# Router products turned round onto 32-column tiles, an older price table for the build-time scheduler, and an earlier start on the first tile's last affine step

## The chip, the cores and the metric

One core of one Trainium2 chip runs the whole network in a single launch. The metric is the device time of that core in microseconds (us), as the median of several runs; the profile is of one execution more. A core has the engines TensorE (PE in the profile, its weight loads PEld), VectorE (DVE), ScalarE (ACT), GpSimd (POOL) and SyncE (SP), which issues most of the DMAs.

## What is computed

The input is `x`, 256 tokens by 1024 numbers. Four layers follow: softmax attention with a dense feed-forward part, a short convolution with a dense feed-forward part, a gated linear recurrence with a mixture of experts, and a stick-breaking attention with a mixture of experts. The two mixtures matter here. For each token the reference computes 20 router logits, picks one of four expert groups and the best two experts in it, and sums these experts' outputs:

```
def post_norm(x, y, g, b):
    return layer_norm(DEEPNORM_ALPHA * x + y.astype(x.dtype), g, b)
...
    probs_g = jax.nn.softmax((xf @ w_group + b_group).astype(jnp.float32), axis=-1)
    p_top, g_idx = lax.top_k(probs_g, 1)
    logits_e = (xf @ w_router + b_router).astype(jnp.float32).reshape(T, N_GROUPS, EXPERTS_PER_GROUP)
...
    h = silu(x @ w_gate) * (x @ w_up);  y = (h * gates) @ w_down
```

After the second mixture comes the last `post_norm`, whose result is the output.

## The kernel before, in words

The 256 tokens are two tiles, T = 0 and T = 1, of 128 each. All weights stream from memory as units of 128 x 1024 numbers (512 KB) into a ring of 34 slots; `pump` (L537) issues their DMAs on SP as slots come free. Weights of dense stages are split by ACT and DVE into a rounded part `hi` and a rest `lo` (`prep_task`), and each product is three matmuls: activations' high part with both, low part with `hi`. The expert weights are used as they come ("raw").

**The order of the work** is made when the program is built. Every stage of each tile is a generator that emits instructions and yields its conditions; `Sched.run` (L269) always resumes the ready generator of lowest priority number, at a time that it keeps itself. That time comes from a table: `mm` (L451) adds a price for a matmul, `tr` (L463) one for a transpose, `onA` and `onD` those of ACT and DVE work, and `pump` says when a unit will have landed, with a fixed distance between units. On the chip nothing of this table is left but the order in which each engine and each DMA queue gets its instructions; an engine runs them in that order and waits on semaphores. So a changed price can move instructions anywhere in the program.

**Router.** `router` (L1370) folds the norm's gain into the router weights, `self.wr` (128 x 8 x 20), and its shift into `self.cr`. When a tile's output projection has made half b of its 1024 columns (`residual_half`, L1274, with a DVE statistics step), `front_half` (L1856) transposes these four blocks of 128, copies them to SBUF on ACT, and multiplies: for each of four blocks the transposed 128 x 128 block is the stationary operand and the 128 x 20 weights move, all eight blocks adding up in one PSUM bank. `moe_front` (L1875) then normalises `x` on DVE, forms the logits from the bank with two DVE steps, chooses the experts, ranks the tokens and builds the selection matrix; then `gather` and the experts' `gate_up` and `down` follow (`moe_task`). Tile 1 goes through its front last, while PE has tile 0's gather and first expert products.

**The end.** `down_last(1, 1)` (L2064) makes the last expert output of tile 1: matmuls, then an ACT copy and a DVE step for its two parts; `combined_last` (L2086) adds them into tile 1's bank. In `moe` (L2135) a tile's final norm begins with DVE statistics of its two banks and a power on POOL (`rstd`). Tile 0 then waits for the event `fin`, which tile 1 sets after its own statistics, and goes through `affine_pool` (L1304): a DVE step for -mean/deviation, two ACT passes of 128 x 512, gain and shift of its first half on POOL (two steps) with a DMA from ACT's queue, and after the event `sent` the same of its second half on DVE with a DMA from SP. Tile 1 uses `affine_rows` (L1289): four DVE steps of 128 x 512, and two DMAs from SP.

Of the kernel before, what the change touches and what calls it, by code (L numbers as in the profile page):

```python
# [8 lines left out]
F32 = mybir.dt.float32  # L9
# [3 lines left out]
ALU = mybir.AluOpType  # L13
# [288 lines left out]
class Body:  # L302
# [148 lines left out]
    def mm(self, out, lhsT, rhs, start, stop, shared=False):  # L451
        self.nc.tensor.matmul(out, lhsT, rhs, start=start, stop=stop, skip_group_check=shared)  # L452
        n = 1
        for d in rhs.shape[1:]:
            n *= d
        m = out.shape[0]
        if lhsT.dtype == F32R:
            c = max(0.227 * n / 512, 0.108)
        else:
            c = max(0.86 * n / 512, 0.224 if m > 64 else 0.112) * (0.26 if m <= 32 and n == 512 else 0.52 if m <= 64 and n == 512 else 1.0)  # L460
        self.sch.now += c

    def tr(self, out, in_):  # L463
        self.nc.tensor.transpose(out, in_, self.ident)  # L464
        self.sch.now += 0.109

    def act(self, out, in_, func, bias=0.0, scale=1.0, accum_out=None):
        want = {AF.Exp: "natural_log_exp_and_others", AF.Ln: "natural_log_exp_and_others", AF.Silu: "silu_and_others"}.get(func)
# [68 lines left out]
    def pump(self):  # L537
        while self.can_dma():
            i = self.nextdma
            if i == 4 and not self.again:  # L540
                self.nc.sync.dma_start(self.x[0], self.x_d[0])
                self.dma_t += 1.46
                self.x0_t = self.dma_t + 2.0
            if i == 18 and not self.again:
                self.nc.sync.dma_start(self.x[1], self.x_d[1])
                self.nc.sync.dma_start(self.cst, self.consts_d[:, 128:])
                self.dma_t += 2.3
                self.x1_t = self.dma_t + 2.0
            if self.plan.kind[i] == "row":
                t = self.ring.tile([128, 1024], F32, tag="u", name="row")  # L550
                r = self.rows_d[self.where[self.plan.src[i]]]
                self.nc.sync.dma_start(t, bass.AP(tensor=r.tensor, offset=r.offset, ap=[[0, 128], [1, 1024]]))
            else:
                t = self.ring.tile([128, 1024], F32, tag="u", name="raw")
                self.nc.sync.dma_start(t, self.units_d[self.where[self.plan.src[i]]])
            self.tiles[i] = t
            self.dma_t = max(self.dma_t, self.sch.now) + 1.3
            self.arr[i] = self.dma_t + 2.0
            if self.plan.kind[i] != "dense":
                self.ready[i] = self.arr[i]  # L560
            self.raw_used += 1
            if self.plan.kind[i] == "dense":
                self.rawdense += 1
            self.nextdma += 1
# [65 lines left out]
    def setup(self):  # L630
        nc = self.nc
        c = self.const
# [13 lines left out]
        self.stat = [c.tile([128, 4], F32, name=f"stat{t}") for t in range(2)]  # L646
        self.gtr = [c.tile([128, 32], F32R, name=f"gtr{t}") for t in range(2)]
        self.bns = [c.tile([128, 12], F32, name=f"bns{t}") for t in range(2)]
        self.wr = c.tile([128, 8, 20], F32, name="wr")
        self.cr = c.tile([128, 40], F32, name="cr")  # L650
        self.sel4 = c.tile([128, 1], F32, name="sel4")
        nc.gpsimd.memset(self.sel4, 0.0)
# [651 lines left out]
    def affine_pool(self, T, nm, src):  # L1304

        x, sv = self.x[T], self.stat[T]
        rows = self.rows(nm)
        yield [self.unit(r) for r in rows]
        nb = self.tm(1)
        self.ts(nb, sv[:, 0:1], sv[:, 2:3], -1.0, ALU.mult, ALU.mult)  # L1310
        for b in range(2):
            c = slice(b * 512, (b + 1) * 512)
            self.act(x[:, c], src[b], AF.Identity, bias=nb, scale=sv[:, 2:3])
        ops = list(zip((ALU.mult, ALU.add), [self.tiles[r] for r in rows]))
        for op, r in ops:
            self.nc.gpsimd.tensor_tensor(x[:, :512], x[:, :512], r[:, :512], op)
        self.nc.scalar.dma_start(self.out_d[T][:, :512], x[:, :512])
        yield f"sent{nm}"
        for op, r in ops:
            self.tt(x[:, 512:], x[:, 512:], r[:, 512:], op)  # L1320
        self.send(T, slice(512, 1024))
        for r in rows:
            self.done(r)
# [46 lines left out]
    def router(self, layer):  # L1370

        g, b_ = self.lncols(f"m{layer}")
        yield [self.bk(1), self.rH(1)]
        h = self.tH()
        t = h[:, :160].rearrange("p (k n) -> p k n", k=8)
        W = h[:, 160:320].rearrange("p (k n) -> p k n", k=8)
        self.nc.gpsimd.dma_start(h[:, 160:320], self.vecs_d[:, V_R + 160 * layer:V_R + 160 * layer + 160])
        yield 5.0
        self.tt(self.wr, W, g.unsqueeze(2).to_broadcast([128, 8, 20]), ALU.mult)
        self.tt(t, W, b_.unsqueeze(2).to_broadcast([128, 8, 20]), ALU.mult)  # L1380
        q = h[:, 320:360]
        self.red(q[:, :20], self.wr.rearrange("p k n -> p n k"), ALU.add)
        self.red(q[:, 20:], t.rearrange("p k n -> p n k"), ALU.add)
        yield self.w()
        bank = self.bank()
        self.mm(bank[:, :20], self.cst[:, C_NONE:C_NONE + 128], q[:, :20], True, True)
        self.mm(bank[:, 20:40], self.ones.bitcast(F32), q[:, 20:], True, True)
        self.vcopy(self.cr[:, :20], bank[:, :20])
        self.tt(self.cr[:, 20:], bank[:, 20:40], self.vecs[:, V_RB + 20 * layer:V_RB + 20 * layer + 20], ALU.add)
        self.free()  # L1390
        self.fH()
# [464 lines left out]
    def front_half(self, T, b, layer):  # L1856

        if b == 0:
            yield [self.bk(2), self.rS(1), ("t", self.ut[T][b])]
            self.xT[T] = self.tS().rearrange("p (k t) -> p k t", k=8)  # L1860
            self.lgb[T] = self.bank()
        else:
            yield [f"fh{layer}_{T}_0", self.bk(1), ("t", self.ut[T][b])]
        xT, lgb = self.xT[T], self.lgb[T]
        bank = self.bank()
        for j in range(4):
            self.tr(bank[:, j * 128:(j + 1) * 128], self.x[T][:, (4 * b + j) * 128:(4 * b + j + 1) * 128])
        self.scopy(xT[:, 4 * b:4 * b + 4].rearrange("p a b -> p (a b)"), bank)
        self.free()
        yield self.w()  # L1870
        for k in range(4 * b, 4 * b + 4):
            self.mm(lgb[:, :20], xT[:, k], self.wr[:, k], k == 0, k == 7)
        self.sch.set(f"fh{layer}_{T}_{b}")

    def moe_front(self, T, layer):  # L1875
# [15 lines left out]
            self.pump()  # L1891
        yield ("t", tl)
        lg = self.tm(20)
        self.stt(lg, self.cr[:, :20], sv[:, 0:1], bank[:, :20], ALU.mult, ALU.add)
        self.stt(lg, lg, sv[:, 2:3], self.cr[:, 20:], ALU.mult, ALU.add)
        self.free()
        gts, mk = self.gts[:, T], self.mks[:, T]
# [237 lines left out]
    def moe(self, T, layer):  # L2135
# [12 lines left out]
            self.onD(512)  # L2148
        self.stats(T, st)
        if T == 0 and self.last[T]:  # L2150
            yield f"fin{layer}"
            yield from self.affine_pool(T, f"f{layer}", acc)
        else:
            self.sch.set(f"fin{layer}")
            yield from self.affine_rows(T, f"f{layer}", acc)
            self.sch.set(f"sentf{layer}")
        self.free(2)
# [125 lines left out]
```

## Time and profile before

| | |
|---|---|
| median of 3 runs | 1204.48 us (1203.82 to 1207.32) |
| profiled execution, its own time | 1204.19 us |
| its span, first to last instruction | 1202.4 us |
| mean granted TensorE clock | 0.988 of full speed |
| busy: PE, DVE, ACT, POOL | 1144.9, 725.0, 549.1, 44.8 us |
| read and written | 298.83 and 2.10 MB |

Busy time of an engine is the union of its instructions; a matmul's record reaches from its start to the (modelled) end of its result, so neighbours overlap, and the pace of PE is read from the distance of two starts. "128*64" in a row is the part of the array that an instruction uses. What stands in brackets at the end of a row is the idle time just before it and what ended it.

### The profile page before, as it was taken

How to read it: one execution, taken by the hardware profiler on the slowest of the kernel's cores; microseconds unless marked ns; L12 is line 12 of the kernel's file. 1: busy time of each engine (PE TensorE's matmuls, PEld its weight loads, DVE VectorE, ACT ScalarE, POOL GpSimd, SP SyncE). 2: the span in 40 equal slices, each digit the busy share in tenths (PEclk: the TensorE clock that was granted, in tenths of full speed). 3: DMA queues.
4: the chain of work that ended last, by engine and by line, in shares of the span. 5: the costliest groups of instructions: out<-in, count | busy, mean ns of one | idle time of the engine just before them, and what ended most of it. 6: DMA issues, size and time to landing. Idle time of an engine off the chain costs nothing. (4 is left out here: it accounts for less than half of the span.)

```text
span 1202.4 us, 16685 instructions
## 1 busy us (share of the span) xinstructions
PE 1144.9 (95%) x6344; PEld 823.7 (69%) x6344; DVE 725.0 (60%) x1121; ACT 549.1 (46%) x913; POOL 44.8 (4%) x65
## 2 busy tenths in 40 slices
PE   7999989999998999999999999999999899999995
PEld 4777768888886787788887789886333577673331
DVE  4577667667577987665556567678221766564214
ACT  4655465434446455544434484553121456631211
POOL 0021000000000000000000000100000100000001
PEclk9999999999999999999999999999999899999998
DMA  9976768777664866466556233377999842587994
GB/s 375 409 306 228 256 222 302 262 268 269 244 239 155 340 247 215 158 211 217 205 194 209 86 125 105 123 277 266 378 409 408 311 142 72 188 333 306 408 408 159
DMA packets 83544, 301.72 MB, mean 251 GB/s; under 512 B 9408, under 2 KB 9824, under 8 KB 83456
## 3 DMA queue, kind: packets, MB, share of 16 engines
q1 hardware_dynamic: 82224, 298.37, 67.1%
q0 software_dynamic: 944, 1.82, 0.6%
q8 instruction: 52, 0.85, 0.3%
q10 hardware_dynamic: 288, 0.38, 0.1%
q14 instruction: 36, 0.29, 0.1%
HBM read 298.83 MB, written 2.10 MB: 250 GB/s over the span
## 5 line engine op out<-in xcount | busy, mean ns | idle before, releaser
L452 PE MATMUL bk<-hi,tS 128*128 128x512 f32 (+1 forms) x1760 | 586.9, 399 | 13.7 <-ACT hi L506 8.0
L452 PEld LDWEIGHTS bk<-hi,tS 128*128 128x128 f32 x1760 | 332.6, 190 | 87.2 <-ACT hi L506 8.7
L487 DVE TENSOR_TENSOR lo<-raw,hi 128x1024 fp32r<-128x1024 f32 x266 | 317.1, 1221 | 67.4 <-ACT hi L506 65.7
L452 PE MATMUL bk<-lo,tS 128*128 128x512 f32 (+1 forms) x880 | 345.0, 392 | 1.6 <-DVE lo L487 1.6
L506 ACT CAST hi<-raw 128x1024 fp32r<-128x1024 f32 x263 | 265.0, 1049 | 20.8 <-DMA raw<-in_units_dram 8.2
L452 PEld LDWEIGHTS bk<-lo,tS 128*128 128x128 f32 x880 | 167.4, 190 | 35.0 <-DVE lo L487 3.4
L480 ACT ACTIVATE tH<-bk 128x256 f32<-128x256 f32 (+1 forms) x100 | 44.8, 449 | 253.8 <-PE bk L452 253.6
L452 PE MATMUL bk<-hi,tH 128*128 128x512 f32 x384 | 133.1, 397 | 1.4 <-ACT tH L506 1.4
L487 DVE TENSOR_TENSOR tH<-tH,bk 128x256 f32<-128x256 f32 x60 | 25.1, 419 | 143.4 <-ACT tH L480 143.3
L452 PE MATMUL bk<-raw,tB 128*32 128x512 f32 x768 | 89.1, 594 | 0.4 <-DVE tB L494 0.4
L452 PEld LDWEIGHTS bk<-hi,tH 128*128 128x128 f32 x384 | 72.3, 189 | 17.1 <-ACT tH L506 2.1
L452 PE MATMUL bk<-raw,tH 128*32 128x512 f32 x640 | 80.1, 594 | 0.6 <-DMA raw<-in_units_dram 0.5
L452 PE MATMUL bk<-lo,tH 128*128 128x512 f32 x192 | 75.1, 391 | 0.0
L498 DVE SCALAR_TENSOR_TENSOR tS<-raw,cs,tS 128x1024 f32<-128x1024 f32 x52 | 66.6, 1280 | 0.3
L452 PEld LDWEIGHTS bk<-raw,tB 128*32 128x32 f32 x768 | 23.2, 110 | 52.4 <-issue 45.9
L498 DVE SCALAR_TENSOR_TENSOR tS<-bk,gsl,tS 128x512 fp32r<-128x512 f32 x32 | 23.3, 749 | 56.2 <-ACT tS L480 55.8
L464 PE MATMUL bk<-identr,tH 128*128 128x128 f32 x296 | 49.9, 277 | 6.8 <-DVE tH L487 3.0
L452 PEld LDWEIGHTS bk<-raw,tH 128*32 128x32 f32 x640 | 22.1, 109 | 49.0 <-issue 39.8
L464 PEld LDWEIGHTS bk<-identr,tH 128*128 128x128 f32 x296 | 36.1, 140 | 28.1 <-issue 8.2
L506 ACT CAST tH<-bk 128x256 fp32r<-128x256 f32 (+1 forms) x52 | 18.5, 356 | 67.5 <-PE bk L464 65.3
L480 ACT ACTIVATE tS<-bk,gsl 128x512 fp32r<-128x512 f32 x32 | 21.1, 686 | 60.7 <-PE bk L452 60.7
L506 ACT COPY tH<-bk 128x256 f32<-128x256 f32 (+1 forms) x56 | 25.6, 474 | 49.0 <-PE bk L452 38.6
(197 smaller groups left out, 990.8 us busy)
## 6 DMA issues: line engine op xcount, KB each, us to landing
raw<-in_units_dram SPq DMA_DIRECT2D x556, 512.0 KB, 5.7
row<-in_rows_dram SPq DMA_DIRECT2D x9, 512.0 KB, 7.6
x<-in_x_dram SPq DMA_DIRECT2D x2, 512.0 KB, 9.6
xsave<-x POOLq DMA_DIRECT2D x2, 512.0 KB, 5.0
out_dram<-x SPq DMA_DIRECT2D x3, 256.0 KB, 2.0
ulv<-in_ulv_dram POOLq DMA_DIRECT2D x1, 384.0 KB, 7.2
cst<-in_consts_dram SPq DMA_DIRECT2D x1, 274.0 KB, 11.2
out_dram<-x ACTq DMA_DIRECT2D x1, 256.0 KB, 2.0
```

Source lines behind the costliest of these rows:

```text
L452: self.nc.tensor.matmul(out, lhsT, rhs, start=start, stop=stop, skip_group_check=shared)
L464: self.nc.tensor.transpose(out, in_, self.ident)
L480: self.nc.scalar.activation(out, in_, func, scale=scale)
L487: self.nc.vector.tensor_tensor(out, a, b, op)
L498: self.nc.vector.scalar_tensor_tensor(out, a, s, b, op0, op1)
L506: self.nc.scalar.copy(out, a)
```

## The change

The router weights get 12 columns of zeros (`self.wr` is 128 x 8 x 32, zeroed by POOL at the start). In `front_half` the weights become the stationary operand, on a tile of 32 columns each, and the transposed block of 128 tokens moves; blocks 0 to 3 and again 4 to 7 go to four groups of 32 PSUM partitions. After the second half a new ACT copy (128 x 128) and a new PE transpose turn the sums back, and `moe_front` adds the four groups with a new DVE reduction. In the scheduler's table, prices of matmuls, of a transpose and the distance between units are replaced. At the end, tile 0 runs its -mean/deviation step and its two ACT passes before it waits for `fin`, and its first DVE step of the second half before it waits for `sent`.

```
@@ mm
         if lhsT.dtype == F32R:
-            c = max(0.227 * n / 512, 0.108)
+            c = 0.216 * max(n, 512 if n < 256 else n) / 512
         else:
-            c = max(0.86 * n / 512, 0.224 if m > 64 else 0.112) * (0.26 if m <= 32 and n == 512 else 0.52 if m <= 64 and n == 512 else 1.0)
+            c = max(0.858 * n / 512, 0.11) * (0.26 if m <= 32 and n == 512 else 0.53 if m <= 64 else 1.0)
@@ tr
-        self.sch.now += 0.109
+        self.sch.now += 0.07
@@ pump
-            self.dma_t = max(self.dma_t, self.sch.now) + 1.3
+            self.dma_t = max(self.dma_t, self.sch.now) + 1.46
@@ setup
-        self.wr = c.tile([128, 8, 20], F32, name="wr")
+        self.wr = c.tile([128, 8, 32], F32, name="wr")
+        nc.gpsimd.memset(self.wr, 0.0)
@@ affine_pool
             self.act(x[:, c], src[b], AF.Identity, bias=nb, scale=sv[:, 2:3])
+        yield f"fin{nm}"
         ops = list(zip((ALU.mult, ALU.add), [self.tiles[r] for r in rows]))
         for op, r in ops:
             self.nc.gpsimd.tensor_tensor(x[:, :512], x[:, :512], r[:, :512], op)
         self.nc.scalar.dma_start(self.out_d[T][:, :512], x[:, :512])
-        yield f"sent{nm}"
         for op, r in ops:
             self.tt(x[:, 512:], x[:, 512:], r[:, 512:], op)
+            yield f"sent{nm}"
@@ router
+        wr = self.wr[:, :, :20]
-        self.tt(self.wr, W, g.unsqueeze(2).to_broadcast([128, 8, 20]), ALU.mult)
+        self.tt(wr, W, g.unsqueeze(2).to_broadcast([128, 8, 20]), ALU.mult)
...
-        self.red(q[:, :20], self.wr.rearrange("p k n -> p n k"), ALU.add)
+        self.red(q[:, :20], wr.rearrange("p k n -> p n k"), ALU.add)
@@ front_half
-            self.mm(lgb[:, :20], xT[:, k], self.wr[:, k], k == 0, k == 7)
+            self.mm(lgb[32 * (k % 4):32 * (k % 4) + 32, :128], self.wr[:, k], xT[:, k], k < 4, k >= 4)
+        if b:
+            yield [self.bk(1), self.rH(1)]
+            t = self.tH()
+            self.scopy(t[:, :128], lgb[:, :128])
+            self.free()
+            yield self.w()
+            self.lgb[T] = self.bank()
+            self.tr(self.lgb[T][:, :128], t[:, :128])
+            self.fH()
@@ moe_front
-        self.stt(lg, self.cr[:, :20], sv[:, 0:1], bank[:, :20], ALU.mult, ALU.add)
+        self.red(lg, bank[:, :128].rearrange("p (g n) -> p n g", g=4)[:, :20], ALU.add)
+        self.stt(lg, self.cr[:, :20], sv[:, 0:1], lg, ALU.mult, ALU.add)
@@ moe
         if T == 0 and self.last[T]:
-            yield f"fin{layer}"
             yield from self.affine_pool(T, f"f{layer}", acc)
         else:
-            self.sch.set(f"fin{layer}")
+            self.sch.set(f"finf{layer}")
```

## Rows read from the trace of the kernel before

**Rows 1.** The page, part 1: engine, busy us (share of span), instructions.

```profile
PE 1144.9 (95%) x6344; PEld 823.7 (69%) x6344; DVE 725.0 (60%) x1121; ACT 549.1 (46%) x913; POOL 44.8 (4%) x65
```

**Rows 2.** Windows table: length, busy (count) by engine, PEclk, DMA share, GB/s.

```profile
0.00:15.00 15.00, 7.25 (x20) 5.45 (x21) 6.54 (x10) 7.85 (x9) 1.89 (x15) 1.00 0.89 341
...
165.00:180.00 15.00, 12.20 (x52) 9.91 (x51) 9.41 (x13) 7.77 (x14) 1.61 (x3) 0.89 0.52 178
...
870.00:885.00 15.00, 15.00 (x132) 4.79 (x128) 2.82 (x4) 3.07 (x6) 0.00 (x0) 1.00 1.03 409
...
945.00:960.00 15.00, 13.77 (x53) 10.30 (x52) 13.63 (x17) 8.07 (x10) 2.81 (x4) 0.78 0.64 237
...
1185.00:1200.00 15.00, 3.70 (x21) 1.09 (x20) 10.11 (x18) 2.14 (x3) 4.36 (x4) 0.68 0.20 73
```

**Rows 3.** Timeline around a change to half-width array tiles: start, us, instruction, idle before.

```profile
808.90 0.39 PE L452 MATMUL bk<-lo,tS 128*128 128x512 f32 x1
...
809.13 0.40 PE L452 MATMUL bk<-hi,tS 128*128 128x512 f32 x1
...
809.46 0.42 PEld L452 LDWEIGHTS bk<-tH,mv 128*64 128x64 f32 x8 [0.36 <-issue]
...
810.05 0.97 PEld L452 LDWEIGHTS bk<-wr,tS 128*128 128x128 f32 x8 [0.17 <-issue]
```

**Rows 4.** Groups of PE by form: count, busy us, mean ns, idle before.

```profile
L464 PE MATMUL bk<-identr,tH 128*128 128x128 f32 x296 | 49.9, 277 | 6.8 <-DVE tH L487 3.0 <-ACT tH L506 3.0 <-ACT hi L506 0.7
...
L452 PE MATMUL bk<-wr,tS 128*128 128x20 f32 x64 | 7.9, 259 | 0.7 <-ACT tS L506 0.7
```

**Rows 5.** Timeline, tile 1's second router half, first mixture, then second mixture.

```profile
825.73 1.07 PE L452 MATMUL bk<-wr,tS 128*128 128x20 f32 x8 [0.68 <-ACT tS L506]
...
826.23 0.80 DVE L494 TENSOR_SCALAR x<-x,stat 128x1024 f32<-128x1024 f32 x1
...
826.95 0.22 DVE L498 SCALAR_TENSOR_TENSOR tm<-cr,stat,bk 128x20 f32<-128x20 f32 x1
...
1073.37 0.99 PE L452 MATMUL bk<-wr,tS 128*128 128x20 f32 x8
...
1074.20 2.98 PE L452 MATMUL bk<-ulv,tS 128*128 128x512 f32 x12
...
1074.30 0.81 DVE L494 TENSOR_SCALAR x<-x,stat 128x1024 f32<-128x1024 f32 x1
...
1075.02 0.23 DVE L498 SCALAR_TENSOR_TENSOR tm<-cr,stat,bk 128x20 f32<-128x20 f32 x1
```

**Rows 6.** Timeline: a 128 x 128 ACT copy and a small DVE reduction, both out of PSUM.

```profile
797.10 0.27 ACT L506 CAST tH<-bk 128x128 fp32r<-128x128 f32 x1
...
1085.30 0.18 DVE L510 TENSOR_REDUCE tm<-bk 128x1 f32<-128x32 f32 x1
```

**Rows 7.** Timeline of the end, from tile 1's last expert output on.

```profile
1187.04 0.15 DVE L494 TENSOR_SCALAR tm<-stat 128x1 f32<-128x1 f32 x1
...
1187.17 0.69 ACT L480 ACTIVATE tS<-bk,gsl 128x512 fp32r<-128x512 f32 x1 [2.40 <-PE bk L452]
1187.33 0.55 POOL L521 TENSOR_TENSOR stat<-tm,mhalf 128x1 f32<-128x1 f32 x1 [113.58 <-DVE tm L494]
1187.89 0.75 DVE L498 SCALAR_TENSOR_TENSOR tS<-bk,gsl,tS 128x512 fp32r<-128x512 f32 x1 [0.70 <-ACT tS L480]
...
1190.59 1.45 ACT L484 ACTIVATE x<-bk,tm,stat 128x512 f32<-128x512 f32 x2 [2.73 <-DVE tm L494]
...
1191.44 3.34 POOL L1316 TENSOR_TENSOR x<-x,row 128x512 f32<-128x512 f32 x2 [0.38 <-ACT x L484]
...
1192.69 0.97 DVE L498 SCALAR_TENSOR_TENSOR x<-x,stat,row 128x512 f32<-128x512 f32 x1
1193.59 2.47 DVE L487 TENSOR_TENSOR x<-x,row 128x512 f32<-128x512 f32 x2
```

**Rows 8.** DVE instructions reading a gain or shift row from 1193.4 us on: min/median/max ns.

```profile
L487 DVE TENSOR_TENSOR x<-x,row x2: 691/1218/1744, 1193.6 to 1195.4; 128x512 f32<-128x512 f32 x2
```

## The prediction

> **What bounds the kernel now.** I read the page's busy times first, then the table of windows of 15 us, then the timeline at the three places that the diff touches. PE is busy for 1144.9 of the span's 1202.4 us [rows 1], so 57.5 us are open to any change of order. They lie unevenly. The first window has 7.75 us of PE idle time and the last stretch, from 1185 us to the end, 17.4 - 3.7 = 13.7 us; that leaves 57.5 - 7.75 - 13.7 = 36 us in all other places together [rows 1, 2]. Within the expert stages the 16 DMA engines are full: 409 GB/s [rows 2] is 524,288 bytes each 1.28 us, and there a unit of weights sets the pace. At changes of stage PE has gaps and then a lower granted clock, 0.89 in one window and 0.78 in another [rows 2]. The reader is to see three kinds of place: dense stages, where PE is the bound and every PE microsecond counts; expert stages, where DMA is; and the end, where PE has finished and DVE, ACT and POOL finish the norm.
>
> **1. The router products.** There are 2 mixtures x 2 tiles x 2 halves = 8 halves of four products, 64 PE instructions in all [rows 4], eight to a half. From the first of eight to the first instruction behind them is 0.83 us at the second mixture [rows 5]. The new half is also eight instructions, with 32 columns of weights and 128 moving. No row has this form. The nearest are the eight of 128 moving columns on tiles of 64: they come behind a matmul that starts at 809.13, whose successor in a dense run would start 0.23 us later (808.90 to 809.13), at 809.36; the next load after the eight starts at 810.05 [rows 3]. So eight cost 0.69 us, of which the loads are busy 0.42, and 0.17 is an idle wait behind them before full-width work goes on [rows 3]. With 32 columns the loads can only be shorter; without their 0.42 some 0.27 would stay. I take 0.60, nearer to the measured 0.69 than to 0.27, because the waits at both ends remain: 0.83 - 0.60 = 0.23 us saved in each half. The bounds are 0.14 and 0.56.
> The Trainium skill, "TensorEngine Tiling (Array Packing)", Theoretical Speedup, gives up to four times for a dimension of 32 or less; an estimate by that page is 8 x 0.83 x 3/4 = 5.0 us saved. The same page, Key Properties, says that a change of tiling mode drains TensorE, which speaks against this change; the idle 0.36 and 0.17 us in the rows agree with that.
> Each front also gets an ACT copy, a PE transpose and a DVE reduction. The copy is 0.27 us, the reduction 0.18 (its 80 inputs lie beyond that row's 32, so up to 0.25) [rows 6], a transpose's result takes 0.277 us, and as PE throughput 49.9/296 = 0.17 [rows 4].
> **Tile 0** goes through its front while PE has tile 1's projection. Copy and reduction are covered by that. Four halves save 4 x 0.23 = 0.92, two transposes cost 0.34: -0.6 us. If the cover were gone, they would cost what tile 1's do.
> **Tile 1, first halves**, also in the projection: -2 x 0.23, -0.45 us.
> **Tile 1, second halves** are a chain that PE soon waits for. First mixture: products from 825.73, + 0.60, + 0.1 handover, + 0.27 copy, + 0.1, + 0.28 transpose, + 0.1 = 827.2; DVE is at its normalisation of x until 827.03; the reduction ends at 827.4, where the first logit step began at 826.95 [rows 5]: +0.45. Second mixture: the transpose is back at 1073.37 + 1.45 = 1074.8, DVE is busy until 1075.1, so only the reduction is added: +0.2. The handovers of 0.1 are an estimate between 0.03 (ACT's copy to DVE's step, [rows 7]) and 0.17 [rows 3]. The copy waits on ACT for the products, and tile 0's gather passes stand behind it; the transpose stands on PE behind gather products. A bound is another 0.8 us (one such pass) in each.
> Router sum: -0.6 - 0.45 + 0.65 = **-0.4 us**, bounds -4 and +2. Zeroing the weights on POOL is covered: POOL has 1.89 us of work in the first 15 us [rows 2] and the tile is next written by the router task, stages later; uncovered it would be at most some 2 us of start.
>
> **2. The end.** The order can be read from the code. Tile 0's generator has a lower priority number than the expert task. As soon as its banks are complete it emits statistics, power, the -mean/deviation step and, since `fin` is no longer asked for first, both ACT passes, before the expert task emits tile 1's last ACT copy. ACT runs in order. So the copy that ran at 1187.17 now stands behind two passes of 1.45 us in all, and these wait for the power on POOL, which ends at 1187.33 + 0.55 = 1187.88 [rows 7]. Worked out: step on DVE (0.15, as its like at 1187.04) until 1188.07, ACT passes 1188.17 to 1189.62, copy from 1189.65: **2.5 us late**. Behind it in line are the DVE step of 1187.89, tile 1's last two matmuls, its statistics, its power and its four DVE steps, all of which set the end. What is won: the -mean/deviation step, 0.15 us, is out of DVE's last stretch. The first DVE product of tile 0's second half moves ahead of tile 1's four steps; DVE has the same steps in the last stretch all the same, and ends with the same one. POOL's two steps (3.34 us) stay behind `fin`, begin after tile 1's power and so overlap tile 1's DVE steps as before.
> In this stretch DVE is slowed while POOL works: one of the two 128x512 products took 1744 ns against 691, one step 0.97 against 0.75 [rows 7, 8], together 1.3 us. I leave these as they are. The end: +2.5 - 0.15 = **+2.3 us**. Bounds: were the copy emitted first and the overlap gone, -0.15 - 1.3 = -1.4; with a second 1744 ns case, +3.4.
> The Trainium skill, "SBUF — State Buffer", states that a DVE instruction with two SBUF inputs and a GpSimd one that reads SBUF exclude each other for the whole instruction. The first product, from 1193.59 and 1.74 us long, ended some 0.6 us after POOL's end at 1191.44 + 3.34 = 1194.78, which is about its 0.69 us alone: that agrees. By the rule alone tile 1's second and fourth step, both with two SBUF inputs, would each wait for one POOL step, up to 1.67 - 0.75 = 0.9 us: 1.8 us in place of 1.3, and an end of +2.8.
>
> **3. The table.** A price changes no instruction, only the order everywhere. The dense matmul is priced at 0.216 where the trace has 0.23 [rows 3] and the old table 0.227; a unit is said to take 1.46 us where the full DMA engines take 1.28 [rows 2] and the old table 1.3. So the planner will believe PE early and weights late: it puts other work in front of matmuls whose weights are already there. Late belief also leaves slack against stalls. The nearest rows for its price are the open 36 us: a gain can't exceed them, and a loss can be as much. I take **0**, since neither sign follows from a row, and carry -9 to +9 us, a quarter of the open time each way.
>
> **Sum.** -0.4 + 2.3 + 0 = +1.9 us on the profiled execution's 1204.19 us (span 1202.4 and 1.8 around it): 1206.1. The median of the runs shown lies 0.3 above that execution, so **1206.4 us**.
>
> **Rivals.** About 0.3% (3.6 us) is what a measurement of this kernel can tell from no change.
> (a) *The other order fills PE's gaps.* If a quarter of the 36 us goes, the time is 1206.4 - 9 = 1197. For: they are many short waits at stage changes, where order is free. Against: the new prices are further from the trace. Chance 0.25.
> (b) *Late belief opens stage changes*, the rival on the slower side. At the step from experts to the next projection a window runs at 0.78 of the clock with PE idle for 1.2 us, costing 0.22 x 15 + 1.2 = 4.5 us; at 165 us, 0.11 x 15 + 2.8 = 4.5 us [rows 2]. If the planner emits the weights' splits later there, since it thinks that they land later, ACT and DVE stand before other work and PE waits. One more gap of this size gives 1206.4 + 4.5 = 1211, two 1215; one is enough to decide. Chance 0.25.
> (c) *The products cost their lower bound and the copy keeps its place.* Router -4 instead of -0.4, end -1.4 instead of +2.3: 1206.4 - 3.6 - 3.7 = 1199. Against: the waits around narrow tiles before and behind narrow tiles [rows 3]. Chance 0.08.
> (d) *Tile 1's front and the end both at their bad bounds*: 1206.4 + 2.4 + 1.1 = 1210. Chance 0.06.
> (e) *The change doesn't do what it says*: "first tile early" makes the last tile late. That is in my forecast.
>
> **How the numbers follow.** The forecast, a net effect of order within some 3 us, has 0.36, all of it within 0.3%. Faster: (a) and (c), 0.33. Slower: (b) and (d), 0.31. The range reaches into (a) and (b) to leave out 1 in 10 on each side: 1194 to 1216. The forecast's own range is 1202 to 1208.
>
> **What would show it.** Right: the eight instructions of a half, start to next full-width load, in 0.5 to 0.7 us; a reduction ahead of the first logit step, 0.2 to 0.5 us later after the products; ACT's two passes of tile 0 from 1188.2 on by the clock of before, and tile 1's last copy directly behind them; tile 1's statistics some 2.5 us later behind its last expert matmul. Wrong: the copy ahead of the passes; windows of 15 us that differ by over 5 us of PE idle time between the two kernels, which would make the table the cause of what is seen.

## The result, and the profile after

The changed kernel takes **1217.33 us** (median of 4 runs, 1216.62 to 1219.13) against 1205.66 for the kernel before on the same chip: a ratio of 1.0100, 95% interval 1.0084 to 1.0116. The forecast was 1206.4, no change within 0.3%, with a range to 1216.0: wrong by 10.9 us, and the time lies just above the range. (Of the kernel before there are now four runs; 1204.48 was the median of the first three.) The profiled execution of after took 1216.94 us with a span of 1215.2, 12.8 more than before's span.

The page, part 1, answers to [rows 1]:

```profile
PE 1146.6 (94%) x6348; PEld 820.3 (68%) x6348; DVE 724.5 (60%) x1127; ACT 547.8 (45%) x915; POOL 46.2 (4%) x66
```

PE's busy time has grown by 1.7 us of the 12.8. The rest is idle time, so the question is which waits are new. To find the stages I use one instruction as a milestone: each norm has a power on POOL, tile by tile, at the same place of the program in every kernel. Its start, and the start of the last cast on DVE, give this table (us; the last line is the span itself; "held" is run e13 below):

| from, to | before | after | table alone | router alone | end alone | held |
|---|---|---|---|---|---|---|
| start, to layer 1's last norm | 479.06 | 477.57 | 477.26 | 479.24 | 477.62 | 476.15 |
| layer 2, to tile 0's first router front | 335.50 | 343.90 | 344.19 | 335.53 | 335.50 | 337.12 |
| to tile 1's front | 11.02 | 10.22 | 9.51 | 10.87 | 11.04 | 9.48 |
| first mixture, to tile 0's next norm | 115.85 | 119.16 | 117.23 | 119.24 | 117.85 | 117.25 |
| layer 3, to tile 1's front | 131.77 | 129.80 | 132.41 | 130.97 | 131.57 | 130.91 |
| second mixture, to tile 0's last norm | 114.13 | 116.67 | 113.17 | 114.99 | 114.47 | 112.99 |
| end, to the last cast | 8.64 | 10.45 | 8.64 | 8.63 | 10.61 | 8.63 |
| behind it | 6.43 | 7.43 | 6.49 | 6.53 | 7.34 | 6.97 |
| span | 1202.4 | 1215.2 | 1208.9 | 1206.0 | 1206.0 | 1199.5 |

One profile of a stage repeats to some 2 us: "end alone" has before's program in its first stages, and still 477.62 for 479.06 and 117.85 for 115.85. What stands out of that is layer 2, +8.4 us, which the table alone has too, and the first mixture, +3.3, which the router alone has. The second mixture's +2.5 is near that limit. The end, +1.8, which the end alone has, is below it, but that row repeats to 0.01 us wherever the order of the end is the same. (What follows the cast is between 6.4 and 7.6 us in the runs below, with and without the new end; I make nothing of it.)

**Layer 2.** The windows of after, then those of before (columns as in [rows 2]):

```profile
756.00:790.00 34.00, 28.35 (x169) 25.14 (x167) 20.58 (x31) 15.57 (x22) 3.61 (x4) 0.90 0.47 156
790.00:822.00 32.00, 28.63 (x164) 22.19 (x165) 21.16 (x40) 14.31 (x35) 0.53 (x1) 1.00 0.61 207
765.00:780.00 15.00, 14.83 (x71) 13.05 (x72) 3.48 (x7) 4.68 (x7) 1.07 (x1) 0.79 0.30 98
```

```profile
756.00:790.00 34.00, 31.03 (x185) 27.14 (x185) 23.28 (x35) 18.30 (x29) 3.62 (x4) 1.00 0.49 171
790.00:822.00 32.00, 31.90 (x200) 26.50 (x199) 21.93 (x51) 14.20 (x34) 0.56 (x1) 1.00 0.74 262
765.00:780.00 15.00, 15.00 (x89) 13.21 (x88) 9.40 (x13) 9.41 (x13) 2.26 (x3) 1.00 0.46 155
```

PE loses 2.7 us of work in the first stretch and 3.3 in the second, and in the first it also runs at a granted clock of 0.90. (After is 1.5 us ahead where layer 2 begins, so the windows don't hold quite the same work. From milestone to milestone PE idles 12.9 us in after and 7.1 before: 5.8 of the 8.4 us.) The timeline of DVE and PE in after shows the first loss; the second fence is before at the same place:

```profile
760.45 0.57 DVE L514 COPY_PREDICATED tS<-masks,bk 128x384 f32<-128x384 uint8 x1
760.92 2.35 DVE L487 TENSOR_TENSOR lo<-raw,hi 128x1024 fp32r<-128x1024 f32 x2
763.18 1.00 DVE L514 COPY_PREDICATED tS<-masks,bk 128x384 f32<-128x384 uint8 x1
...
764.48 0.55 DVE L487 TENSOR_TENSOR tB<-tB,tS 128x384 f32<-128x384 f32 x1
...
759.02 1.55 PE L452 MATMUL bk<-tS 128*128 128x128 f32 x12
765.17 2.90 PE L452 MATMUL bk<-tB,tS 128*128 128x128 f32 x12 [4.60 <-DVE tB L487]
```

```profile
758.74 1.68 DVE L514 COPY_PREDICATED tS<-masks,bk 128x384 f32<-128x384 uint8 x2
...
760.72 0.54 DVE L487 TENSOR_TENSOR tB<-tB,tS 128x384 f32<-128x384 f32 x1
...
764.41 4.63 DVE L487 TENSOR_TENSOR lo<-raw,hi 128x1024 fp32r<-128x1024 f32 x4 [2.19 <-ACT hi L506]
...
761.41 1.58 PE L452 MATMUL bk<-tB,tS 128*128 128x128 f32 x12 [2.51 <-DVE tB L487]
```

Before, DVE does the recurrence's last steps of tile 1 in a row, and the weights' splits (`lo`) 3 us later. After, two splits, 2.35 us, stand between them. PE has nothing else queued and waits 4.60 us in place of 2.51; then the granted clock is at its lower level, 1.2 GHz (0.50 over these 2.90 us), and the same 12 products take 2.90 us in place of 1.58. This wait has 2.1 of the 5.8 us; the rest are shorter ones behind it, the longest 1.7 us.

**Router.** The timeline of PE and its loads in after, tile 0's second half inside a dense run; under it the group of the new products, whose columns are those of [rows 4]:

```profile
822.30 0.40 PE L452 MATMUL bk<-hi,tS 128*128 128x512 f32 x1
822.62 0.16 PEld L452 LDWEIGHTS bk<-tS,wr 128*32 128x32 f32 x8 [0.36 <-issue]
...
822.98 0.42 PEld L464 LDWEIGHTS bk<-identr,x 128*128 128x128 f32 x4 [0.20 <-DVE bns L1282]
```

```profile
L452 PE MATMUL bk<-tS,wr 128*32 128x128 f32 x64 | 3.4, 285 | 1.3 <-ACT tS L506 1.3
```

Counted as in the prediction, the eight cost 0.45 us: a dense matmul would follow at 822.30 + 0.23 = 822.53, the next load starts at 822.98. PE's products are 3.4 us of busy time in place of 7.9 [rows 4]. But tile 1's logits come late. The timeline behind tile 1's second half, which answers to [rows 5]:

```profile
831.84 0.43 PE L452 MATMUL bk<-tS,wr 128*32 128x128 f32 x8 [0.67 <-ACT tS L506]
832.33 0.27 ACT L506 COPY tH<-bk 128x128 f32<-128x128 f32 x1 [0.55 <-PE bk L452]
832.34 0.80 DVE L494 TENSOR_SCALAR x<-x,stat 128x1024 f32<-128x1024 f32 x1
...
833.29 0.41 PE L464 MATMUL bk<-identr,tH 128*128 128x128 f32 x1
...
834.60 0.81 DVE L494 TENSOR_SCALAR tB<-bk,vecs 128x512 f32<-128x512 f32 x1 [1.46 <-PE bk L452]
835.33 0.23 DVE L510 TENSOR_REDUCE tm<-bk 128x20 f32<-128x80 f32 x1
835.60 0.24 DVE L498 SCALAR_TENSOR_TENSOR tm<-cr,stat,tm 128x20 f32<-128x20 f32 x1
```

The first logit step is 835.60 - 831.84 = 3.76 us behind the products, where before it was 1.22 [rows 5]. Copy and transpose are through by 833.70; DVE could reduce then, but a pass over tile 0's gathered tokens (`tB`) stands ahead in DVE's order and waits 1.46 us for its own product. In the second mixture it is 3.64 us for 1.65.

Tile 0's step is late as well. In the first mixture it is 2.84 us behind the second half's products, before 2.24; in the second it is 5.13 us for 1.00 (after, then before, second mixture):

```profile
1069.19 0.43 PE L452 MATMUL bk<-tS,wr 128*32 128x128 f32 x8
...
1072.72 0.69 DVE L498 SCALAR_TENSOR_TENSOR x<-x,bk 128x512 f32<-128x512 f32 x1 [3.25 <-PE bk L452]
...
1074.06 0.22 DVE L510 TENSOR_REDUCE tm<-bk 128x20 f32<-128x80 f32 x1
1074.32 0.24 DVE L498 SCALAR_TENSOR_TENSOR tm<-cr,stat,tm 128x20 f32<-128x20 f32 x1
```

```profile
1061.18 0.96 PE L452 MATMUL bk<-wr,tS 128*128 128x20 f32 x8
...
1062.18 0.23 DVE L498 SCALAR_TENSOR_TENSOR tm<-cr,stat,bk 128x20 f32<-128x20 f32 x1 [0.60 <-PE bk L452]
```

A residual step of tile 1 (`x`) stands ahead of the reduction there and waits 3.25 us for its own product. Tile 0's gather then begins behind tile 1's last router products (1081.46 and 1080.73); before, four of its products ran ahead of them (1072.37 and 1073.37). Runs e2, e8, e12 and e17 have the same 5.12 or 5.13 us; what it costs wasn't tried by itself.

**The end.** The timeline of after, which answers to [rows 7]:

```profile
1197.32 0.55 POOL L521 TENSOR_TENSOR stat<-tm,mhalf 128x1 f32<-128x1 f32 x1 [115.60 <-DVE tm L494]
...
1198.21 1.45 ACT L484 ACTIVATE x<-bk,tm,stat 128x512 f32<-128x512 f32 x2 [3.46 <-DVE tm L494]
1199.55 0.68 ACT L480 ACTIVATE tS<-bk,gsl 128x512 fp32r<-128x512 f32 x1
1200.27 0.75 DVE L498 SCALAR_TENSOR_TENSOR tS<-bk,gsl,tS 128x512 fp32r<-128x512 f32 x1 [2.15 <-ACT tS L480]
...
1202.71 0.68 DVE L487 TENSOR_TENSOR x<-x,row 128x512 f32<-128x512 f32 x1
1202.93 0.86 POOL L521 TENSOR_TENSOR stat<-tm,mhalf 128x1 f32<-128x1 f32 x1 [5.07 <-DVE tm L494]
...
1203.77 2.93 POOL L1318 TENSOR_TENSOR x<-x,row 128x512 f32<-128x512 f32 x2
1204.14 1.43 DVE L498 SCALAR_TENSOR_TENSOR x<-x,stat,row 128x512 f32<-128x512 f32 x1
...
1207.17 0.68 DVE L487 TENSOR_TENSOR x<-x,row 128x512 f32<-128x512 f32 x1
```

Tile 1's last copy stands behind both passes: it starts 2.23 us behind tile 0's power, where before it started 0.16 ahead of it [rows 7]. From the last 16 expert products (1195.08) to the cast (1207.77) it is 12.69 us, before 10.87.

### The profile page after: what moved, and what is told of

It is laid out like the page before. It is cut to its first block, busy times and chain, and to the rows that moved or that the text cites. A ratio compares the mean times of both kernels' runs of the same rounds, so it can differ in the third digit from the quotient of the medians.

```text
span 1215.2 us, 16682 instructions
## 1 busy us (share of the span) xinstructions
PE 1146.6 (94%) x6348; PEld 820.3 (68%) x6348; DVE 724.5 (60%) x1127; ACT 547.8 (45%) x915; POOL 46.2 (4%) x66
## 5 line engine op out<-in xcount | busy, mean ns | idle before, releaser
L506 ACT CAST hi<-raw 128x1024 fp32r<-128x1024 f32 x261 | 262.1, 1049 | 9.3 <-DMA raw<-in_units_dram 8.9
L487 DVE TENSOR_TENSOR tH<-bk,tH 128x256 fp32r<-128x256 f32 (+1 forms) x52 | 20.6, 400 | 48.4 <-ACT tH L506 48.4
L506 ACT COPY tH<-bk 128x256 f32<-128x256 f32 (+2 forms) x60 | 27.1, 461 | 46.3 <-PE bk L452 38.6
```

Of the source, the lines that this page charges most:

```text
L487: self.nc.vector.tensor_tensor(out, a, b, op)
L506: self.nc.scalar.copy(out, a)
```

## The experiments

Ratios are to the kernel before, run beside each on the same chip, with 95% intervals.

**The parts alone.** Runs e1, e2 and e3 each have one part of the diff: the four price edits; the router (with its zeroed weights); the end. Run e4 is the end with one more edit, so that tile 0's last norm waits until tile 1's last ACT copy is emitted:

```diff
         if T == 0 and self.last[T]:
+            yield f"yl{layer}_1_1"
             yield from self.affine_pool(T, f"f{layer}", acc)
```

> The kernel before with the changed table alone. By the theory that the table costs the most, tile 0's power on POOL in the first mixture's front comes at about 821 us as in the changed kernel (814.56 before), and the kernel is 5 to 8 us slower. By the rival that the router products shift the order and the table is harmless, that power stays within 1 us of 814.6 and the time within 2 us of the kernel before.

Measured 1.0033 (1.0020 to 1.0047). The loss lies in layer 2 (table above), and PE's wait there is the 4.60 us of after.

> The kernel before with the new router products alone. By the theory, everything up to 810 us stays as before; then the products of tile 1's second halves start earlier, but its first logit step stands 2 to 2.5 us later behind them than before (1.22 and 1.65 us there), since a gather pass of tile 0 comes between them on DVE: +2 to +4 us in all. By the working of the prediction the chain grows by 0.45 and 0.2 us and the sum is -0.4 us; by the rival of the first run the kernel is 6 us or more slower.

Measured 1.0014 (1.0004 to 1.0023). Tile 1's logit step is 825.79 to 829.81 = 4.02 us behind its products in the first mixture; that mixture is 3.4 us longer than before, the second 0.9.

> The kernel before with the new end alone. By the theory, ACT's two passes stand ahead of tile 1's last copy, and the time from the last expert products (1185.10 before) to the cast of the flag grows from 10.87 us to 12.7, +1.8 us. By the rival that the earlier start pays, it shrinks by about 1 us.

Measured 1.0021 (1.0011 to 1.0031); last expert products to cast 12.84 us.

> The new end with one wait more: tile 0's -mean/deviation step and its ACT passes are emitted once tile 1's last copy and DVE step are. By the theory that the order on ACT is the whole cost, the stretch of 10.87 us shrinks to between 9.5 and 10.3: the copy is not late, the small step is out of DVE's last stretch, and the slowed product of 1744 ns is gone. By the rival that POOL's overlap or DVE's order costs as much, it stays at 11 us or above.

Measured 0.9999 (0.9990 to 1.0009); last expert products to cast 10.40 us, 0.47 less than before. In its timeline the copy is ahead of the passes:

```profile
1188.73 0.69 ACT L480 ACTIVATE tS<-bk,gsl 128x512 fp32r<-128x512 f32 x1 [2.39 <-PE bk L452]
...
1191.02 1.45 ACT L484 ACTIVATE x<-bk,tm,stat 128x512 f32<-128x512 f32 x2 [1.60 <-DVE tm L494]
```

So the end's loss is the place of one copy: 12.84 - 10.40 = 2.4 us, and the rest of the new order is worth 0.5.

**Which price.** Runs e5, e6, e9 and e10 have one price edit of the change each: in this order the unit's, the dense matmul's, the transpose's and that of matmuls that aren't float32r. Run e7 has the last two together, and e11 moves the transpose's price as far the other way, to 0.148.

```diff
-            self.dma_t = max(self.dma_t, self.sch.now) + 1.3
+            self.dma_t = max(self.dma_t, self.sch.now) + 1.46
-            c = max(0.227 * n / 512, 0.108)
+            c = 0.216 * max(n, 512 if n < 256 else n) / 512
-        self.sch.now += 0.109
+        self.sch.now += 0.07
-            c = max(0.86 * n / 512, 0.224 if m > 64 else 0.112) * (0.26 if m <= 32 and n == 512 else 0.52 if m <= 64 and n == 512 else 1.0)
+            c = max(0.858 * n / 512, 0.11) * (0.26 if m <= 32 and n == 512 else 0.53 if m <= 64 else 1.0)
```

> The kernel before with one price changed: the distance between units, 1.46 for 1.3. By the theory that believing weights late opens the gaps, the power of tile 0's first front, at 814.56 before and 821.45 with the whole table, comes at 818 or later, and PE's 4.6 us wait near 760 us is seen. By the rival that the dense price does it, that power stays within 1.5 us of 814.6 and the time within 2 us.

Measured 0.9996 (0.9986 to 1.0005). PE's wait in layer 2 is 2.50 us as before and the clock 1.00. The order isn't the one of before: some 420 of PE's 6344 products stand at another place. So a unit believed later does move work, and by itself costs nothing; rival (b)'s cause falls.

> The kernel before with the dense matmul's price alone, 0.216 for 0.227. By the theory that PE's clock running 5 per cent ahead in the planner does the harm, tile 0's power comes at 818 us or later, with the wait of 4.6 us near 760 us. By the rival that the unit's price does it, within 1.5 us of 814.6.

Measured 1.0029 (1.0014 to 1.0043), a loss, with tile 0's first front 2.7 us later than before. Of that 2.4 us are there at layer 1's last norm already (481.50); layer 2 is 335.79 us long.

> The kernel before with the other prices alone: unrounded float matmuls and transposes. By both theories little happens: tile 0's power within 1.5 us of 814.6, the time within 2 us. By a third theory, that any reshuffling of the order costs about the same, it is as late as with the whole table.

Measured 1.0059 (1.0040 to 1.0077), the largest loss of a part, and it isn't in layer 2. Layer 1's last norm comes at 486.42 us, 7.4 later than before; layer 2 then takes 334.91 us, with 2.51 us of waiting at the recurrence's step as before. The new wait is at the end of layer 1, where the longest of before is 1.81 us (timeline, DVE, then PE):

```profile
461.93 2.35 DVE L487 TENSOR_TENSOR lo<-raw,hi 128x1024 fp32r<-128x1024 f32 x2
...
465.52 1.22 DVE L487 TENSOR_TENSOR lo<-raw,hi 128x1024 fp32r<-128x1024 f32 x1
466.66 0.69 DVE L487 TENSOR_TENSOR tB<-tB 128x512 f32<-128x512 f32 x1
...
468.05 0.79 PE L452 MATMUL bk<-hi,tS 128*128 128x512 f32 x1 [5.04 <-ACT tS L506]
```

Three splits stand ahead of the step (`tB`) from which ACT makes what PE waits for: the picture of layer 2 at another place. That these splits make the wait is read from the rows and wasn't tried.

> Only the planner's price of a transpose: 0.07 us in place of 0.109; no instruction changes. The two prices together with the float32 one cost 0.59% and moved tile 0's first expert front of layer 2 from 814.56 to 821.33. Theory 1, the transposes: a third less time is believed in the recurrence's transposes, so work that should fill that wait is put elsewhere; then this kernel alone shows 820 to 822 at that front and a ratio of 1.004 to 1.007. Theory 2, the float32 price: then this kernel is within 0.15% of the kernel before and the next one carries the loss. Theory 3, any reshuffle costs about as much: both show 1.002 to 1.006.

Measured 1.0056 (1.0043 to 1.0070). Its loss is at e7's place: PE waits there for a norm's step, layer 1's last norm comes at 485.49 us, and layer 2 takes no longer than before (332.40).

```profile
467.51 1.94 PE L464 MATMUL bk<-identr,tS 128*128 128x128 f32 x8 [5.48 <-DVE tS L492]
```

> Only the planner's price of a matmul that is not float32r: products of fewer than 131 columns on more than 64 rows are priced at 0.11 to 0.22 in place of 0.224, those of 33 to 64 rows at 0.53 of the whole at every width. Theory 1 (transposes): within 0.15% of the kernel before, first expert front of layer 2 at 814 to 816. Theory 2 (this price): 1.004 to 1.007, that front at 820 to 822. Theory 3 (any reshuffle): 1.002 to 1.006.

Measured 1.0055 (1.0042 to 1.0068), and here the waits of PE from 756 to 822 us begin with the one of after (columns: us in total, times, longest):

```profile
PE bk L452 <- DVE tB L487: 4.6, 1, 4.6
```

Four splits, 4.61 us, stand ahead of the step here, and layer 2 takes 343.40 us.

> The planner's price of a transpose moved as far the other way: 0.148 us in place of 0.109. If the direction of the new price is what harms (work put in front of a PE that is believed early), a dearer transpose costs nothing or gains: ratio 0.996 to 1.001. If any reshuffle of this order costs about as much, this one is slower as well: 1.002 to 1.006, with the loss in layer 2's stretch or another like it.

Measured 1.0015 (1.0006 to 1.0024). So neither one price nor one direction does it: the cheaper transpose and the float32 price cost 0.55% each, at two different places, and together no more than one alone; the dearer transpose loses as well, though less. Of the three theories only the third, any reshuffle, is left, and not in full, since e5's new order costs nothing: a new order can cost 0.15 to 0.6%, each through waits of its own. Alone, only the float32 price has the 4.60 us of the whole change. That doesn't show yet that the splits make this wait.

**The wait itself.** Run e13 is the table alone with a rule that keeps `prep_task` from emitting splits from the recurrence's last products of tile 1 to its last DVE step; e14 is the whole changed kernel with it:

```diff
-                if self.hold or self.arr[i] is None or j > self.dense_pos + self.AHEAD or self.hl_used + 2 > self.hl_max() or self.raw_used + self.hl_used + self.s_used + 2 > self.N:
+                if self.hold or self.wait2 or self.arr[i] is None or j > self.dense_pos + self.AHEAD or self.hl_used + 2 > self.hl_max() or self.raw_used + self.hl_used + self.s_used + 2 > self.N:
...
-                yield [("t", tdone[l] + 0.12), self.bk(1)]
+                self.wait2 |= T == 1 and quad == 1 and l == nl - 1; yield [("t", tdone[l] + 0.12), self.bk(1)]
...
-                self.SMIN = 10
+                self.SMIN, self.wait2 = 10, False
```

> The table alone, and one rule more: no split of weights is emitted between the recurrence's last products of tile 1 and its last step on DVE; with the former table this rule changes nothing. Theory, the splits stand ahead: the two of 1.18 us each are gone from in front of DVE's step that PE waits for, PE's wait falls from 4.60 to 2.2 to 2.6 us, the clock in the window from 765 to 780 stays at 0.95 or more in place of about half, and the first expert front of layer 2 comes 3 to 4 us earlier, at 817 to 818.5; ratio 1.000 to 1.002 where the table alone had 1.0033. Rival, the splits are needed as soon: PE then waits for the splits themselves a few us later, the gaps of 0.4 to 1.7 us between 776 and 821 grow by as much, and the front stays at 820 to 822; ratio 1.0025 to 1.0045.

Measured **0.9982** (0.9970 to 0.9994): faster than before, clear of 1, though by less than the 0.3% that the prediction called the least that can be told. Its timeline at the same place, DVE, then PE, and under it the window (columns as in [rows 2]):

```profile
758.91 1.68 DVE L514 COPY_PREDICATED tS<-masks,bk 128x384 f32<-128x384 uint8 x2
...
760.89 0.54 DVE L487 TENSOR_TENSOR tB<-tB,tS 128x384 f32<-128x384 f32 x1
...
765.87 2.36 DVE L487 TENSOR_TENSOR lo<-raw,hi 128x1024 fp32r<-128x1024 f32 x2 [3.48 <-ACT hi L506]
...
761.58 2.90 PE L452 MATMUL bk<-tB,tS 128*128 128x128 f32 x12 [2.54 <-DVE tB L487]
...
765.00:780.00 15.00, 14.54 (x89) 12.79 (x89) 11.88 (x14) 11.63 (x14) 2.26 (x3) 1.00 0.50 178
```

The wait is 2.54 us again and the clock is back at full by 765. Tile 0's first front comes at 813.27, 8.2 us earlier than with the table alone; 1.1 of that was there already at 479 us, so layer 2 gives back 7.1 us where I expected 3 to 4. The wait's own share is 4.60 - 2.54 = 2.06 us, and the lower clock is over sooner; what remains came with the order behind the held splits, which the rule changes too, and isn't separated from them. PE's idle time in layer 2 is 7.9 us again, where the table alone has 12.4 and the kernel before 7.1. The rule with the former table has no run, so the gain over the kernel before belongs to table and rule together.

> The whole changed kernel with the same rule. Theory: 3 to 4 us less than the changed kernel, so a ratio of 1.006 to 1.008 to the kernel before in place of 1.010, the router's and the end's losses staying. Rival: 1.009 to 1.0115.

Measured 1.0032 (1.0020 to 1.0044), 0.68% less than the changed kernel and lower than expected, with tile 0's first front at 814.23 in place of 821.47. So the largest loss of the change goes when these splits are held back, in the part and in the whole.

> Router and end of the change, with the table as it was. If the parts add up: 1.0014 + 1.0021 of the two alone give 1.0035 (1.0025 to 1.0045), and the table's share of the whole is then 0.65%, twice its own 0.33%. If router and end hurt each other: 1.005 to 1.008, and the table's share stays at 0.33%.

Measured 1.0042 (1.0029 to 1.0055): router and end add up (0.14 + 0.21%). What the table adds to them is 1.0100 - 1.0042 = 0.58%, some 7 us, as the two profiles have it (1215.2 - 1208.0); its own 0.33% by the medians is 4 us, by the profiles 6.5. Here the profiled execution of e1 is 1.5 us above the median of its runs and that of before 0.8 below, which makes up the difference. With the intervals as they are, one size of the table's loss for both isn't excluded.

**The router's wait.** Run e8 is e2 with one of tile 0's gather passes, the one ahead of the reduction, given to ACT:

```diff
-            self.affine(dk % 2 == 0, self.xg[T][dk], bank, A[:, dk:dk + 1], B[:, dk:dk + 1])
+            self.affine(dk % 2 == 0 or (T == 0 and dk == 1), self.xg[T][dk], bank, A[:, dk:dk + 1], B[:, dk:dk + 1])
```

> The new router products alone, with tile 0's one gather pass that stands on DVE ahead of tile 1's reduction moved to ACT. By the theory that this pass is the loss, tile 1's first logit step comes 1.7 to 2.3 us after its second half's products began (4.0 with the pass in front, 1.22 in the kernel before), and the first expert stage from tile 1's power to tile 0's next one is 1.5 to 2 us shorter than the 119.2 us with the pass. By the rival that the copy and the transpose are the loss, the step stays at 3.5 us or more.

Measured 1.0004 (0.9994 to 1.0014). The reduction now follows DVE's normalisation:

```profile
825.60 0.80 DVE L494 TENSOR_SCALAR x<-x,stat 128x1024 f32<-128x1024 f32 x1
826.67 0.24 DVE L510 TENSOR_REDUCE tm<-bk 128x20 f32<-128x80 f32 x1 [0.27 <-PE bk L464]
```

The first logit step is 1.85 and 2.02 us behind the products, and the first mixture is 117.15 us, 2.1 shorter than in e2. So the pass made tile 1's step late. In time e8 is 0.10% below e2, with intervals that overlap: how much of the router's loss the pass was isn't settled.

**Versions.** Run e12 has the table of before, the end of e4, and the narrow products for tile 0 alone; e16 the new table with splits held and the end of e4, with the router of before; e17 is e16 with narrow products for tile 0; e18 is e16 with both tiles and the pass on ACT.

> The parts that paid, together: the end's new order with tile 1's last copy ahead of tile 0's passes, and the narrow router products for tile 0 alone; the table as before. Theory: the end gives 0.5 us (10.87 to 10.40 measured), tile 0's four halves save some 0.35 us each and cost two transposes of 0.17: 1.0 us; tile 1's logit steps stand as before, 1.2 and 1.7 us behind its products. Ratio 0.998 to 1.0. Rival: the new instructions shift the planner's order again and it lands at 1.001 to 1.004.

Measured 1.0000 (0.9991 to 1.0010), as e4 without narrow products (0.9999): they gain nothing here.

> New table, splits held, the end with tile 1's last copy first; router products as before. Theory: 0.9982 of the table with held splits less the 0.5 us of the end (0.04%): 0.9970 to 0.9985; last expert products to flag cast in 10.2 to 10.6 us. Rival: the end gives nothing, 0.9980 to 0.9995.

Measured **0.9972** (0.9960 to 0.9983), 0.28% below the kernel before: the fastest that was tried.

> The same with narrow router products for tile 0 alone. Theory: another 1 us (0.08%) less: 0.9962 to 0.9980; tile 1's first logit steps 1.2 and 1.7 us behind their products. Rival: the order moves again and takes it back, 0.998 to 1.002.

Measured 1.0010 (1.0000 to 1.0019): the rival. In the second mixture's front of e17 DVE has four gather passes in a row after its choice of tile 1's experts, where e16 has two (first e17, then e16):

```profile
1079.30 2.96 DVE L494 TENSOR_SCALAR tB<-bk,vecs 128x512 f32<-128x512 f32 x4
```

```profile
1079.70 1.52 DVE L494 TENSOR_SCALAR tB<-bk,vecs 128x512 f32<-128x512 f32 x2
```

That mixture is 115.27 us long against 113.03, though tile 1's products are the old ones. Tile 0's logit step is 5.12 us behind its products, in e16 1.00.

> The same with narrow products for both tiles and the gather pass on ACT. Theory: within 0.05% of the version with tile 0 alone, since tile 1's first halves save 0.35 us each and its logit steps come 0.4 us later. Rival: tile 1's chain costs its 0.5 to 1 us in each mixture and nothing hides it: 0.05 to 0.15% above that version.

Measured 1.0003 (0.9994 to 1.0013), a little below e17, which neither theory said. Narrow products cost 0.3 to 0.4% in both versions with the new table. Neither the gather passes nor tile 0's late step is shown to be the cause: e12 has both, with the former table, and costs no more than e4.

## Why the prediction was wrong

**What bounds the kernel** held: of the 12.8 us between the two profiles 11.1 are idle time of PE, and the new waits that were found lie at changes of stage, in the fronts and at the end.

**The table** is the step that failed. I took 0, "since neither sign follows from a row", with bounds of 9 us either way; it measured +4 alone and +7 within the change, inside the bounds and with a sign. One thing was to be had from rows: the wait of 2.51 us for the recurrence's step, with PE's queue empty and splits of 1.18 us each that can be put ahead of that step. I read only windows there, and took both signs from the open 36 us; but what an order can lose isn't measured by the idle time that is open to it, it is the work that can get ahead of a step for which PE waits. The sign was not to be had from rows. Five of the six price runs lost and the sixth, e5, moved work and gained nothing clear, so after the fact the chance of 0.25 for a faster order looks too high. The sign set for the table, windows of 15 us that differ by over 5 us of PE idle time, was too coarse: before the last one no two differ by more than 2.7.

**Rival (b)** had the picture, splits ahead of other work on DVE, a longer PE wait and a lower clock. Its cause, a unit believed late, costs nothing alone (e5); the prices of PE itself do it. And it looked for the gaps at 165 us and at the step out of the experts, where the change has its largest new wait in the recurrence.

**The router**: "0.60 us" for a half measured 0.45, so the saving was larger than I took and within its bounds. The copy (0.27) and the reduction (0.23) are as priced. The term that was mis-sized is tile 1's chain, +0.45 and +0.2: it is 3.76 - 1.22 = +2.5 and 3.64 - 1.65 = +2.0 us. I added durations along the chain and put the gather pass into a bound of 0.8 us; the pass itself waits 1.46 us for PE in front of the reduction, and DVE runs in order. For tile 0 I called copy and reduction covered; in the second mixture they are not, 5.13 us for 1.00, again by a step that waits for PE ahead of the reduction. Measured alone, the router costs 0.14% (1.7 us) for the -0.4 forecast.

**The end** was right in its mechanism and nearly in size: +2.3 forecast, +1.8 in the trace of after, 0.21% (2.5 us) measured alone; the copy starts directly behind the passes. The 1744 ns product [rows 8] is gone, and a step of 1.43 us beside POOL stands in its place, so "I leave these as they are" held in sum.

**The sum**: of the 10.9 us some 7 are the table, 2.1 the router, 0.2 the end, and 1.2 the median of the kernel before, which stood at 1204.48 when the forecast was made and is 1205.66 with the fourth run. Of the three terms none came out lower than taken. That the time lies above the range and not in it is a matter of 1.3 us, as much as that median moved.

## What to carry to other kernels

A price in a static planner is an edit of the whole program: time each price by itself, and look in the trace for long work that the new order puts ahead of a step that PE waits for; a rule that holds such work back gave more here than any of the six price edits. When a step is added to a chain, ask which instruction stands ahead of it on its engine and what that one waits for, not only how long the step is. Give an engine's queue the work that ends the program first, and earlier tiles' work behind it.

## What the runs showed of the hardware

The same idle time doesn't always bring the same clock: behind 2.51 us of waiting the 12 products took 1.58 us in the kernel before, at a granted clock of 1.00, and behind 2.54 us in e13 they took 2.90 at 0.50, the lower level. Nothing in the rows here says why.

A power on POOL of one number per partition takes 0.55 us; beside a DVE product of two SBUF inputs it took 0.86 (1202.93 in after). A DVE step of 0.75 us took 1.43 beside POOL's gain step. The Trainium skill, "SBUF — State Buffer", Summary: rules for kernel authors, says that of a DVE instruction with two SBUF inputs and a GpSimd one that reads SBUF the second to issue blocks until the first finishes; that both instructions are longer agrees. The POOL one ended 0.40 us behind the DVE product (1202.71 + 0.68 = 1203.39), near its 0.55 alone.

Around the eight narrow products the weight loads idle twice, 0.36 us ahead and 0.20 behind (the row puts the second down to DVE; at 816.48 and 1064.39 it is the same 0.20 with `issue` as the reason). The products between need little: 0.45 us for eight where the loads alone are 0.16. The Trainium skill, "TensorEngine Tiling (Array Packing)", Theoretical Speedup, gives up to four times for a dimension of 32 or less; here it is 0.83 / 0.45, less than twice.
